# A hybrid encoder layer: first tiles in a hand-written order, another routing order, and the fourth expert pair's weights loaded in the order in which the first pair leaves its blocks

## The chip, the core and the metric

The kernel runs on one core of one Trainium2 chip. The metric is the device time of one execution in microseconds. The kernel before was timed three times: 592.09, 594.92 and 598.53 us, median 594.92 us. One further execution was profiled, and everything read from the trace is of that one.

## What is computed

512 tokens of 1024 features go through one post-norm encoder layer. What matters here of the reference:

```python
def reference(x, positions, ln_emb_g, ln_emb_b, w_in, ...):
    h = layer_norm(x, ln_emb_g, ln_emb_b)
    proj = h @ w_in[l]
    qa, ka, va, cq, ckv, kr = jnp.split(proj, IN_SPLITS, axis=-1)
    ...
    out_a = windowed_gqa_sink(qa, ka, va, a_sink[l])
    qb = (rms_norm(cq, q_a_norm_g[l]) @ w_q_b[l]).reshape(b, s, B_HEADS, 96)
    kv = (rms_norm(ckv, kv_a_norm_g[l]) @ w_kv_b[l]).reshape(b, s, B_HEADS, 128)
    ...
    out_b = mla_attention(q_nope, q_rope, k_nope, k_rope, v_b)
    mixed = jnp.concatenate([rms_norm(out_a, ...), rms_norm(out_b, ...)], axis=-1) @ w_out[l]
    h = layer_norm(DEEPNORM_ALPHA * h + mixed, ln_attn_g[l], ln_attn_b[l])
    ffn = hierarchical_moe(h, ...)   # 32 experts, each token goes to two of them
    h = layer_norm(DEEPNORM_ALPHA * h + ffn, ln_ffn_g[l], ln_ffn_b[l])
```

An expert is `silu(t @ w_gate[e]) * (t @ w_up[e]) @ w_down[e]` with 256 hidden features: 2 MB of gate and up weights and 1 MB of down weights in float32. All 32 experts are used, so 96 MB of weights are read.

## The kernel before, in words

**Start and projection.** The tokens lie in four tiles of 128 (`z[0]` to `z[3]`). Each is loaded in two halves of 512 features (`load_x`), its mean and variance are taken on DVE (`ln_stats`), and `layer_norm` applies mean, factor, gain and bias in four DVE operations per tile, with gain and bias broadcast over 128 partitions (`lng`, `lnb`, 1 MB together, loaded on SP's queue behind the first tile). PE transposes the tile in two groups of four 128x128 blocks (L257), and `split` makes of each group a rounded high half (`hth`, a cast on ACT, L208) and a low half (`htl`, a subtraction on DVE, L209). A product is three matmuls: high by high, high by low, low by high. The weights `w_in` come in four column chunks; a chunk is four loads of 512 KB (`wf`, L161), split into `wh` (ACT) and `wl` (POOL for the first chunk, DVE for the others). The first chunk's 24 matmuls of tile 0 (L385) take the high weights first; all other tiles use `mm3` (L213 to L215).

**Attention.** The low-rank vectors are expanded to queries, keys and values of the eight MLA heads in two column halves `c` of four tokens' tiles `t` each: `heads` transposes and splits, and L497 and L323 to L332 scale and rotate the queries. Behind them come scores (maximum `bnm` on DVE, L574; exponential `pr` on ACT, L577), values, the output projection, and the second LayerNorm. Up to here a scheduler, which simulates the engines, sets the order of instructions on each engine; priorities given in the source only help it.

**Routing and experts.** From the last part of the output projection on, everything is issued in the order in which it is written (`manual_schedule`). Tiles are handled in the order 0, 1, `a`, `b`; for each: logits (`logits`), choice of experts (`route`), counting (`count`), slots (`place`), selection matrix (`sel0_`), and a matmul that gathers the chosen rows, transposed (`gather`, L1109). The experts run in 16 pairs, 64 slots each, side by side on the array. One pair: 8 blocks `j` of gate and up weights, 16 matmuls in the program (the trace shows two records for each; L1243, `gates`), the activation (`gated`), 8 matmuls of down weights (L1263, `down`), and the result added to the rows `xg`, which a scatter writes to memory (`leave_rows`). The weights lie in a ring of six slots (`RING`); while pair p runs, pair p+3 is loaded into the two slots that p leaves. SP issues these loads in order: first expert's gate and up weights, second's (`load_gus`, L692), then the down weights (L709, L712). In slots 0 and 1 the first half of gate and up weights (blocks 0 to 3) is two tiles of 512 KB and the second half one of 1 MB; in the other slots both halves are 1 MB. The slots 0 and 1 hold the pairs 0, 3, 6, 9, 12 and 15. In pair 0, a group of small matmuls for the first places (L1368) stands behind the first two blocks of the gates. The end takes the last pair's result by a matmul instead of a scatter (L1310), adds the rows that were scattered, and applies the last LayerNorm.

Of the kernel before, what the change touches and what calls it, by code (L numbers as in the profile page):

```python
# [12 lines left out]
F32 = mybir.dt.float32  # L13
# [58 lines left out]
def build(tc, A, out):  # L72
# [24 lines left out]
    with top:  # L97
# [38 lines left out]
        def bvec(pl, src, n, name):  # L136
            t = pl.tile([P, n], F32, name=name)
            SY.dma_start(out=t, in_=src.partition_broadcast(P))
            return t
        load_x(0)  # L140
        lg, lb = [lp.tile([P, D], F32, name=nm) for nm in ("lng", "lnb")]
        for n in range(2):
            for dst, nm in ((lg, "ln_emb_g"), (lb, "ln_emb_b")):
                SY.dma_start(out=dst[:, 512 * n:512 * n + 512], in_=A[nm][512 * n:512 * n + 512].partition_broadcast(P))
        SY.dma_start(out=cst, in_=A["cst"][:, :C_KEEP])

        nch = [-1]

        def chunk_load(pieces):
# [4 lines left out]
            for q in range(4):  # L154
# [10 lines left out]
                split(wf[:, :, :n], wh[:, :, :n], wl[:, :, :n], PO if nch[0] == 0 else V)  # L165
# [32 lines left out]

        def layer_norm(src, dst, g, b):
            mv, rs = ln_stats(src)  # L200
            for i in range(2):
                sl = slice(512 * i, 512 * i + 512)
                V.scalar_tensor_tensor(dst[:, sl], src[:, sl], mv[:, 0:1], g[:, sl], ALU.subtract, ALU.mult)
                V.scalar_tensor_tensor(dst[:, sl], dst[:, sl], rs, b[:, sl], ALU.mult, ALU.add)
# [43 lines left out]
        for t in range(NT):  # L248
            if t == 0:
                chunks.append(chunk_load([(768, 512)]))  # L250
            elif t + 1 < NT:
                load_x(t + 1)
            layer_norm(xs[t], z[t], lg, lb)
            for kk in range(2):
                pt = ptr()
                for k in range(4):
                    PE.transpose(pt[:, k * P:(k + 1) * P],  # L257
                                 z[t][:, (4 * kk + k) * P:(4 * kk + k + 1) * P], ident)
                pv = pt.rearrange("p (a b) -> p a b", a=4)
                o = (slice(None), slice(4 * kk, 4 * kk + 4), slice(t * P, (t + 1) * P))  # L260
                split(pv, hth[o], htl[o])
# [112 lines left out]
        def chunk(ch, first=False):  # L374
            n, hs = ch
            for t in range(NT):
                pp = pproj()
                if first and t == 0:
                    ts_ = slice(t * P, (t + 1) * P)
                    O = []  # L380
                    for q in range(4):
                        O += [(k, a_, 0) for a_ in (hth, htl) for k in (2 * q, 2 * q + 1)]
                    O += [(k, hth, 1) for k in range(NK)]
                    for i, (k, a_, l) in enumerate(O):
                        PE.matmul(pp, a_[:, k, ts_], hs[k // 2][l][:, k % 2], start=(i == 0), stop=(i == 3 * NK - 1))  # L385
                    yield t, pp
                    continue
# [15 lines left out]
        for t, pp in chunk(chunks[0], True):  # L403
# [59 lines left out]
        scr = pool(p2, "p2s", bufs=2, side="right")  # L463

        def heads(src, hi, lo, c, t):
# [4 lines left out]
            split(pt[:96].rearrange("p (a b) -> p a b", a=4), hi[o], lo[o])  # L470

        for c in range(2):
            wh, wl = kv0 if c == 0 else wprep(w2, A["w_kv_b"][0], gkv, 2, 512 * c, 512)
            for t in range(NT):
# [12 lines left out]
        for c in range(2):  # L487
            wh, wl = wprep(w2, A["w_q_b"][0], gq, 6, 384 * c, 384)
            for t in range(NT):
# [9 lines left out]
                heads(qt_, qth, qtl, c, t)  # L499
# [1111 lines left out]
```

## Time and profile before

| what | value |
|---|---|
| median of 3 timed runs | 594.92 us (592.09 to 598.53) |
| the profiled execution, its own time | 591.33 us |
| its span, first to last instruction | 589.5 us |
| busy share of the span: PE, DVE, ACT, POOL | 89%, 55%, 38%, 17% |
| mean granted TensorE clock | 0.970 |

The time of the profiled execution is 1.8 us longer than its span, and the median is 0.6% above it. A busy share is a mean over stages. PE has idle time in the first 20 us, around 155 us, between 320 and 340 us and behind 548 us. A row of the timeline gives the start, the duration of a group of like instructions, the engine, the line, the operation with its output and inputs, and in brackets the idle time of the engine before it with what released it. SPq is SP's queue of DMA issues; its durations are those of the issuing, waits between issues included, not of the transfers.

### The profile page before, as it was taken

What the parts mean: (1) busy time and instruction counts of PE and PEld (TensorE: products, weight loads), DVE (VectorE), ACT (ScalarE), POOL (GpSimd) and SP (SyncE); (2) the same over time, 40 slices, a digit from 0 to 9 for tenths busy, and PEclk for the clock granted to TensorE, in tenths of its full rate; (3) what the DMA queues carried; (4) which work ended last, traced back from release to release, by engine and by line L of the source; (5) the groups of instructions that cost most, each with busy time, mean ns of one, the idle gap of its engine ahead of it and who ended that gap; (6) DMA issues with size and microseconds to landing.
All of it is one profiled execution on the core that took longest, in us unless ns stands there. A gap on an engine that the chain in (4) does not pass through costs nothing. (4 is left out here: it accounts for less than half of the span.)

```text
span 589.5 us, 8004 instructions
## 1 busy us (share of the span) xinstructions
PE 523.4 (89%) x2756; PEld 331.8 (56%) x2757; DVE 322.6 (55%) x882; ACT 222.1 (38%) x477; POOL 99.9 (17%) x141
## 2 busy tenths in 40 slices
PE   2899999999898999999998899999998699979860
PEld 1688898789766777677777444343433234323230
DVE  4946463775688757947768734434524222202177
ACT  2256451564597738856731312111111111101032
POOL 1700221311100000213200201123111101000051
PEclk9999999999899999999999989999999889989985
DMA  8983310221201005991266799999999999999663
GB/s 279 280 290 81 102 43 0 59 81 42 85 16 58 1 1 212 289 367 39 66 258 259 280 391 410 420 415 415 411 417 400 421 418 391 412 420 416 264 267 142
DMA packets 46268, 141.76 MB, mean 240 GB/s; under 512 B 12380, under 2 KB 19420, under 8 KB 37009
## 3 DMA queue, kind: packets, MB, share of 16 engines
q1 hardware_dynamic: 40608, 131.06, 58.5%
q0 software_dynamic: 4464, 8.06, 3.6%
q10 hardware_dynamic: 1152, 2.10, 0.9%
q8 instruction: 23, 0.38, 0.3%
q14 instruction: 21, 0.16, 0.1%
HBM read 133.14 MB, written 16.25 MB: 253 GB/s over the span
## 5 line engine op out<-in xcount | busy, mean ns | idle before, releaser
L1243 PE MATMUL p_gu<-w_gu,xT 128*64 128x512 f32 x512 | 125.0, 613 | 15.0 <-DMA w_gu<-in_w_gu 14.1
L1243 PEld LDWEIGHTS p_gu<-w_gu,xT 128*64 128x64 f32 x512 | 39.6, 141 | 95.6 <-issue 70.0
L1247 ACT ACTIVATE hid<-p_gu 128x256 f32<-128x256 f32 x16 | 6.1, 384 | 176.0 <-PE p_gu L1243 163.9
L1248 DVE TENSOR_TENSOR hid<-hid,p_gu 128x256 f32<-128x256 f32 x16 | 6.7, 421 | 113.9 <-ACT hid L1247 113.8
L1263 PE MATMUL p_y<-w_dn,hidT 128*64 128x512 f32 x256 | 59.9, 611 | 1.0 <-issue 0.6
L1276 DVE SCALAR_TENSOR_TENSOR xg<-p_y,wsl,xg 128x512 f32<-128x512 f32 x30 | 22.5, 751 | 28.4 <-PE p_y L1263 26.5
L1263 PEld LDWEIGHTS p_y<-w_dn,hidT 128*64 128x64 f32 x256 | 17.5, 140 | 31.4 <-issue 29.3
L604 PE MATMUL ptr<-cst,pr 128*128 128x128 f32 x208 | 33.3, 278 | 1.9 <-ACT pr L562 1.4
L1034 POOL DMA_INDIRECT xg<-norm_rows,tok x16 | 16.5, 1032 | 104.5 <-PE p_y L1263 16.8
L1269 POOL DMA_INDIRECT moe_rows<-xg,idx x15 | 15.6, 1039 | 95.0 <-DVE xg L1276 69.6
L604 PEld LDWEIGHTS ptr<-cst,pr 128*128 128x128 f32 x208 | 24.9, 145 | 9.5 <-ACT pr L562 3.2
L577 ACT ACTIVATE pr<-pmm,bnm 128x512 f32<-128x512 f32 x32 | 22.0, 689 | 10.6 <-DVE bnm L574 9.7
L574 DVE TENSOR_REDUCE bnm<-pmm 128x1 f32<-128x512 f32 x32 | 21.9, 687 | 5.3 <-PE pmm L215 4.8
L215 PE MATMUL pmm<-wh,htl 128*128 128x512 f32 (+1 forms) x64 | 24.0, 374 | 0.0
L213 PE MATMUL pmm<-wh,hth 128*128 128x512 f32 (+1 forms) x64 | 23.8, 372 | 0.0
L214 PE MATMUL pmm<-wl,hth 128*128 128x512 f32 (+1 forms) x64 | 23.5, 368 | 0.0
L562 ACT ACTIVATE pr<-pr,rc 128x512 f32<-128x512 f32 (+2 forms) x32 | 20.6, 645 | 4.1 <-DVE rc L560 3.9
L590 DVE CUSTOM_DVE_ANT_0 sm<-pmm,mask,nsink 128x256 f32<-128x256 f32 (+1 forms) x32 | 17.4, 545 | 7.6 <-PE pmm L587 6.5
L215 PE MATMUL pwo<-wh,htl 128*128 128x512 f32 (+1 forms) x56 | 20.7, 370 | 0.0
L214 PE MATMUL pwo<-wl,hth 128*128 128x512 f32 (+1 forms) x56 | 20.5, 367 | 0.0
L213 PE MATMUL pwo<-wh,hth 128*128 128x512 f32 (+1 forms) x56 | 20.5, 367 | 0.0
L1232 ACT ACTIVATE xg<-xg,of 128x1024 f32<-128x1024 f32 x15 | 17.2, 1149 | 8.5 <-PE p_x L1228 7.8
(349 smaller groups left out, 1161.6 us busy)
## 6 DMA issues: line engine op xcount, KB each, us to landing
w_gu<-in_w_gu SPq DMA_DIRECT2D x52, 1024.0 KB
w_dn<-in_w_dn SPq DMA_DIRECT2D x20, 1024.0 KB
w_gu<-in_w_gu SPq DMA_DIRECT2D x24, 512.0 KB
w_dn<-in_w_dn SPq DMA_DIRECT2D x24, 512.0 KB
wf<-in_w_in SPq DMA_DIRECT2D x12, 512.0 KB
moe_rows<-zr SPq DMA_DIRECT2D x8, 512.0 KB
rows<-moe_rows SPq DMA_DIRECT2D x8, 512.0 KB
wf<-in_w_q_b SPq DMA_DIRECT2D x12, 192.0 KB
```

Source lines behind the costliest of these rows:

```text
L213: PE.matmul(ps, ah, bh, start=first, stop=False)
L214: PE.matmul(ps, ah, bl, start=False, stop=False)
L215: PE.matmul(ps, al, bh, start=False, stop=last)
L562: SC.mul(pr[:, :n], pr[:, :n], rc)
L574: V.tensor_reduce(nm, sp, AX.X, ALU.max, negate=True)
L577: exps_.append(SC.activation(pr[:, :S], sp, AF.Exp, bias=nm, accum_out=den).ins)
L590: V.tensor_tensor_reduce(sm[:, :nk], sp[:, :nk], mask[:, mo:mo + nk], 1.0, nsink[:, h:h + 1], ALU.add, ALU.min, nm)
L604: PE.transpose(pt[:, k * P:(k + 1) * P], pr[:, k * P:(k + 1) * P], ident)
L1232: SC.mul(pl["xg"], pl["xg"], pl["of"])
L1243: PE.matmul(pg[64 * i:64 * i + 64], xT[:, j, 64 * i:64 * i + 64], ws[i][0][j], start=(j == 0), stop=(j == 7))
L1263: r = PE.matmul(py[64 * i:64 * i + 64, :], hT[:, j, 64 * i:64 * i + 64], ws[i][1][n][:, j], start=(j == 0), stop=(j == 1))
L1276: V.scalar_tensor_tensor(y, py, pl["wsl"], y, ALU.mult, ALU.add)
```

## The change

The start has other data and another order. Gain and bias of the first LayerNorm come as a small transposed table `geT` (64 bytes per partition) on ACT's DMA queue, with the constants. A tile is only normalised (one ACT operation per half, `scaled_x`), transposed, and gets gain and bias per 128x128 block after the transpose (`gain_x`, on DVE or ACT), into `hf`, from which `high` (ACT) and `low` (DVE) are made. The low halves of the first chunk's weights move from POOL to DVE (`w_low`). Tiles 0 and 1 with their 24 matmuls each stand in a hand-written order:

```diff
-            layer_norm(xs[t], z[t], lg, lb)
...
+        def scaled_x(t, kk):
...
+            SC.activation(z[t][:, sl], xs[t][:, sl], AF.Identity, scale=rs, bias=nb)
...
+        def gain_x(t, kk, ks, eng):
...
+                    SC.activation(hf[:, k], pt[:, k * P:(k + 1) * P], AF.Identity, scale=g_, bias=b_)
...
+                    V.tensor_scalar(hf[:, k], pt[:, k * P:(k + 1) * P], g_, b_, ALU.mult, ALU.add)
...
+        def w_low(q):
+            V.tensor_tensor(chunks[0][1][q][1], wfs[q], f32v(chunks[0][1][q][0]), ALU.subtract)
...
+        with tc.manual_schedule(engines={V.engine, SC.engine, PE.engine, PO.engine}):
+            stats_half(0, 0)
+            stats_half(0, 1)
+            stats_end(0)
+            stats_shift(0)
             for kk in range(2):
...
+                scaled_x(0, kk)
+                turn_x(0, kk)
+            gain_x(0, 0, range(4), V)
+            w_high(0)
...
+            w_high(2)
+            first_mm(0, hth, 2, 0)
+            first_mm(0, htl, 2, 0)
+            for kk in range(2):
+                scaled_x(1, kk)
+                turn_x(1, kk)
```

ACT's rows show the start's order. `hth` is a tile's rounded half, `wh` one of the first chunk's four rounded weights. Before:

```order
L208 CAST hth<-ptr 128x4x128
L208 CAST wh<-wf 128x1024
L208 CAST hth<-ptr 128x4x128
L208 CAST wh<-wf 128x1024 x3
L208 CAST hth<-ptr 128x4x128 x2
```

and now:

```order
L271 ACTIVATE z_64<-xt,ln_nb_158,ln_rs 128x512 x2
L298 CAST wh<-wf 128x1024
L284 ACTIVATE hf<-ptr,geT 128x128
L292 CAST hth<-hf 128x4x128
L284 ACTIVATE hf<-ptr,geT 128x128
L298 CAST wh<-wf 128x1024
L292 CAST hth<-hf 128x4x128
L298 CAST wh<-wf 128x1024
L271 ACTIVATE z_65<-xt,ln_nb_205,ln_rs 128x512 x2
L298 CAST wh<-wf 128x1024
L292 CAST hth<-hf 128x4x128
```

The two halves of tile 0 are now normalised ahead of everything else on ACT, some of the gains stand between the casts, and tile 1's two normalisations (`z_65`) stand between the third and the fourth weight cast.

The z that the later residual needs gets its gain and bias in the query projection. Two loads of 512 KB (`lgb`) are issued on SP's queue at the second half's key projection, and two DVE operations per tile and half stand behind each low half of the queries:

```diff
+                for dst, nm in zip(lgb, ("ln_emb_g", "ln_emb_b")):
+                    SY.dma_start(out=dst, in_=A[nm].rearrange("(a b) -> a b", a=2).partition_broadcast(P))
...
+                with tc.issue_after(heads(qt_, qth, qtl, c, t)):
+
+                    zt = z[t][:, 512 * c:512 * c + 512]
+                    V.tensor_tensor(zt, zt, lgb[0][:, c], ALU.mult)
+                    V.tensor_tensor(zt, zt, lgb[1][:, c], ALU.add)
```

DVE's rows show it at the first scores, where the second half's queries end (`qtl` is a low half of queries, `rp` a rotation, `bnm` the maximum of a row of scores, `rc` and `pr` a softmax's end). Before:

```order
L209 TENSOR_TENSOR qtl<-ptr,qth 96x4x128
L574 TENSOR_REDUCE bnm<-pmm 128x1
L323 SCALAR_TENSOR_TENSOR rp_1615<-pwo,rq_337,ctb 128x128
L331 SCALAR_TENSOR_TENSOR rp_1616<-pwo,rq_337,stb 128x4x16 x2
L209 TENSOR_TENSOR qtl<-ptr,qth 96x4x128
L323 SCALAR_TENSOR_TENSOR rp_1649<-pmm,rq_338,ctb 128x128
L331 SCALAR_TENSOR_TENSOR rp_1650<-pmm,rq_338,stb 128x4x16 x2
L560 RECIPROCAL rc<-den 128x1
L574 TENSOR_REDUCE bnm<-pmm 128x1
L564 TENSOR_SCALAR pr<-pr,rc 128x512
```

and now:

```order
L584 TENSOR_TENSOR qtl<-ptr,qth 96x4x128
L619 TENSOR_TENSOR z_64<-z_64,ln_emb_g 128x512
L695 TENSOR_REDUCE bnm<-pmm 128x1
L441 SCALAR_TENSOR_TENSOR rp_1676<-pwo,rq_426,ctb 128x128
L449 SCALAR_TENSOR_TENSOR rp_1677<-pwo,rq_426,stb 128x4x16 x2
L584 TENSOR_TENSOR qtl<-ptr,qth 96x4x128
L619 TENSOR_TENSOR z_65<-z_65,ln_emb_g 128x512
L620 TENSOR_TENSOR z_64<-z_64,ln_emb_b 128x512
L441 SCALAR_TENSOR_TENSOR rp_1712<-pmm,rq_427,ctb 128x128
L449 SCALAR_TENSOR_TENSOR rp_1713<-pmm,rq_427,stb 128x4x16 x2
L681 RECIPROCAL rc<-den 128x1
L620 TENSOR_TENSOR z_65<-z_65,ln_emb_b 128x512
```

Four operations on z now stand in this stretch, between the maxima on which the exponentials wait; four more follow behind it.

In the routing, the gain and bias of one half of tile `a` move ahead of the logits, `route(a)` is cut into five steps and a rest, and `place`, `count`, `sel0_` and `gather` of tile `a` move back behind `route(b)`; the row numbers and selection of the second group (`rows_of`, `select_tile`) come ahead of the exponentials:

```diff
-        steps(route(a))
-        place(1)
+        ra = route(a)
+        steps(ra, 5)
         turn(b, 0)
```

The first pair's gates go through the blocks in the order 4 to 7, 0 to 3, its places still behind the first two blocks; the factors of the rows (`residual`, `places_weights`) and the transposes for the second pair (`columns`) move between the matmuls of `down` and the DVE operations that take their result:

```diff
         def gu_tiles(slot, i):
-            if i == 0 and slot < 2:
-                return [(f"gu{slot}0{q}", 2 * q, 2) for q in range(2)]
+            if i == 1 and slot < 2:
+                return [(f"gu{slot}1{q}", 4 + 2 * q, 2) for q in range(2)]
             return [(f"gu{slot}{i}", 4 * i, 4)]
...
+        def load_turns(e, slots):
+
+            ws = [{}, {}]
+            for h in (1, 0):
+                for ts in zip(*[gu_tiles(sl, h) for sl in slots]):
+                    for i in range(2):
+                        tag, j, n = ts[i]
+                        ws[i].update(zip(range(j, j + n), load_blocks(e + i, slots[i], tag, j, n)))
...
+                if p == 0:
+                    ws[p + 3] = [(gu, None) for gu in load_turns(e, (s0, s1))]
...
+                order = 4, 5, 6, 7, 0, 1, 2, 3
+                gates(pg, xT, ws[p], order, 0, 2)
+                first_rows()
+                gates(pg, xT, ws[p], order, 2)
...
+            def between():
+
                 for i in range(2):
                     columns(plc[1], i, nx)
+                residual(0)
```

SP's rows show the loads of the fourth pair. A tile of 128x1024 is 512 KB, one of 128x2048 is 1 MB. Before, slot 0's three tiles and then slot 1's three:

```order
L692 DMA w_gu000_3971<-in_w_gu 128x1024
L692 DMA w_gu001_3973<-in_w_gu 128x1024
L692 DMA w_gu01_3975<-in_w_gu 128x2048
L692 DMA w_gu100_3977<-in_w_gu 128x1024
L692 DMA w_gu101_3979<-in_w_gu 128x1024
L692 DMA w_gu11_3981<-in_w_gu 128x2048
```

and now, with the slot as the first digit of the name, the half as the second and the quarter as the third:

```order
L817 DMA w_gu010_4038<-in_w_gu 128x1024
L817 DMA w_gu110_4040<-in_w_gu 128x1024
L817 DMA w_gu011_4042<-in_w_gu 128x1024
L817 DMA w_gu111_4044<-in_w_gu 128x1024
L817 DMA w_gu00_4046<-in_w_gu 128x2048
L817 DMA w_gu10_4048<-in_w_gu 128x2048
```

The two slots now take turns, and the second halves (blocks 4 to 7) come ahead of the first. For the pairs 6, 9, 12 and 15 the loads still go slot by slot, but in each the 1 MB tile is now the first and the two of 512 KB follow.

## Rows read from the trace of the kernel before

**Rows 1.** Windows: us, then busy us (instructions) per engine, PEclk, DMA share, GB/s

```profile
10.00:20.00 10.00, 6.34 (x18) 4.03 (x19) 8.86 (x13) 5.17 (x6) 6.74 (x4) 1.00 0.93 311
60.00:70.00 10.00, 10.00 (x52) 8.26 (x51) 4.08 (x9) 4.40 (x11) 1.37 (x3) 1.00 0.16 46
400.00:500.00 100.00, 90.36 (x428) 35.56 (x423) 32.35 (x90) 14.83 (x21) 15.81 (x15) 0.97 1.01 411
```

**Rows 2.** Timeline 0 to 18 us, DVE, POOL, ACT: start, us, idle before

```profile
5.53 0.15 DVE L181 TENSOR_SCALAR rsq_t<-ln_mv 128x1 f32<-128x1 f32 x1
5.77 0.55 POOL L183 TENSOR_TENSOR ln_rs<-rsq_t,mhalf 128x1 f32<-128x1 f32 x1 [4.56 <-DVE rsq_t L181]
...
8.01 0.75 DVE L203 SCALAR_TENSOR_TENSOR z<-xt,ln_mv,lng 128x512 f32<-128x512 f32 x1 [2.32 <-DMA lng<-in_ln_emb_g]
...
10.41 0.23 DVE L348 CAST identr<-cst 128x128 fp32r<-128x128 f32 x1
...
17.18 1.04 ACT L208 CAST wh<-wf 128x1024 fp32r<-128x1024 f32 x1 [0.30 <-DMA wf<-in_w_in]
```

**Rows 3.** Timeline of PE, 10 to 26 us

```profile
10.53 1.95 PE L257 MATMUL ptr<-cst,z 128*128 128x128 f32 x8 [10.53 <-DMA cst<-cst]
...
13.23 1.22 PE L385 MATMUL pwo<-wh,hth 128*128 128x512 f32 x2 [0.76 <-ACT wh L208]
...
19.75 1.09 PE L257 MATMUL ptr<-cst,z 128*128 128x128 f32 x4 [2.10 <-DVE z L204]
...
24.91 1.09 PE L385 MATMUL pwo<-wl,hth 128*128 128x512 f32 x4
```

**Rows 4.** Costliest groups by form: busy us, mean ns | idle before

```profile
L209 DVE TENSOR_TENSOR wl<-wf,wh 128x1024 fp32r<-128x1024 f32 x8 | 9.9, 1254 | 1.8 <-ACT wh L208 1.8
L484 DVE TENSOR_SCALAR vb<-pwo,rq 128x256 f32<-128x256 f32 x4 | 1.9, 471 | 0.0
L1122 DVE TENSOR_TENSOR z<-z,lngb 128x512 f32<-128x512 f32 x2 | 1.4, 684 | 0.0
...
L208 ACT CAST wh<-wf 128x1024 fp32r<-128x1024 f32 x12 | 12.4, 1056 | 2.2 <-DMA wf<-in_w_in 1.4 <-PE pmm L215 0.3 <-issue 0.3
L1114 ACT ACTIVATE z<-z,ln_nb,ln_rs 128x512 f32<-128x512 f32 x2 | 1.5, 806 | 0.9 <-DVE ln_nb L1119 0.9
```

**Rows 5.** Timeline 156 to 158 us, PE and DVE

```profile
156.47 0.50 PE L213 MATMUL pmm<-kth,qth 96*128 96x512 f32 x1 [1.71 <-ACT pr L577]
...
157.46 0.69 DVE L574 TENSOR_REDUCE bnm<-pmm 128x1 f32<-128x512 f32 x1
```

**Rows 6.** Windows, columns as in rows 1

```profile
130.00:150.00 20.00, 19.97 (x122) 19.37 (x121) 10.93 (x27) 8.78 (x17) 2.60 (x4) 1.00 0.20 59
155.00:160.00 5.00, 3.54 (x15) 2.91 (x16) 4.90 (x14) 2.68 (x8) 0.91 (x2) 0.78 0.54 180
330.00:338.00 8.00, 6.24 (x34) 2.49 (x33) 6.16 (x38) 0.85 (x2) 3.28 (x3) 1.00 0.64 186
342.00:350.00 8.00, 8.00 (x46) 3.67 (x44) 4.11 (x10) 1.63 (x2) 1.02 (x1) 0.99 1.02 399
```

**Rows 7.** Timeline of the first pair, PE, then SP's queue

```profile
326.92 1.94 PE L1243 MATMUL p_gu<-w_gu,xT 128*64 128x512 f32 x8 [0.78 <-DVE gn L892]
...
330.66 5.37 PE L1243 MATMUL p_gu<-w_gu,xT 128*64 128x512 f32 x24
...
328.88 9.21 SPq L692 DMA_DIRECT2D w_gu<-in_w_gu  x6
342.55 3.01 SPq L709 DMA_DIRECT2D w_dn<-in_w_dn  x4
```

**Rows 8.** Timeline of the last pair, SP's queue, then PE

```profile
525.76 12.78 SPq L692 DMA_DIRECT2D w_gu<-in_w_gu  x6
...
548.16 1.02 PE L1243 MATMUL p_gu<-w_gu,xT 128*64 128x512 f32 x2
550.38 7.39 PE L1243 MATMUL p_gu<-w_gu,xT 128*64 128x512 f32 x30 [1.20 <-DMA w_gu<-in_w_gu]
```

More of the change, by code (lines that the diff above doesn't have):

```diff
@@ L139, in bvec @@
             return t
+        geT = cp.tile([P, 2, NK], F32, name="geT")
+        SC.dma_start(out=cst, in_=A["cst"][:, :C_KEEP])
+        SC.dma_start(out=geT, in_=A["ge_T"])
         load_x(0)
[L141 to L145, printed above, removed]
         nch = [-1]
+        wfs = []
         def chunk_load(pieces):
@@ L247, in build @@
         chunks = []
[L248 to L252, printed above, removed]
-            layer_norm(xs[t], z[t], lg, lb)
-            for kk in range(2):
[L255 to L261, printed above, removed]
+        chunks.append(chunk_load([(768, 512)]))
@@ L262, in build @@
+        for t in range(2, NT):
+            for i in range(2):
+                stats_half(t, i)
+            stats_end(t)
+            stats_shift(t)
+            for kk in range(2):
+                scaled_x(t, kk)
+                turn_x(t, kk)
+                if kk:
+                    gain_x(t, kk, range(4), SC)
+                else:
+                    gain_x(t, kk, range(4), V)
+                high(t, kk)
+                low(t, kk)
         lnst.close()
@@ L372, in build, with chunk @@
         scr0, scr, scr1 = [pool(p1, nm, bufs=2, side="right") for nm in ("p1s0", "p1s", "p1s1")]
-        def chunk(ch, first=False):
+        def chunk(ch, first=()):
             n, hs = ch
             for t in range(NT):
+                if t < len(first):
+                    yield t, first[t]
+                    continue
                 pp = pproj()
[L378 to L387, printed above, removed]
                 for k in range(NK):
@@ L1209, in build @@
         for t in (1, a, b):
+            rows_of(t)
+        sels[1] = [select_tile(2, t) for t in range(NT)]
+        for t in (1, a, b):
             exps(t)
@@ L1256, in gated, with down @@
             return hT
-        def down(hT, ws, put):
+        def down(hT, ws, put, between=None):
+            pys = []
             for n in range(2):
@@ L1264, in down @@
                                       ws[i][1][n][:, j], start=(j == 0), stop=(j == 1))
-                put(slice(512 * n, 512 * n + 512), py)
+                pys.append(py)
+                if not between:
+                    put(slice(512 * n, 512 * n + 512), py)
+            if between:
+                between()
+                for n in range(2):
+                    put(slice(512 * n, 512 * n + 512), pys[n])
             return r.ins
@@ L1276, in put @@
                 V.scalar_tensor_tensor(y, py, pl["wsl"], y, ALU.mult, ALU.add)
-            r = down(hT, ws, put)
+            r = down(hT, ws, put, between)
             scatter(pl)
```

207 lines of the change are left out of this document (145 added, 62 removed).

## The prediction

> **What bounds the kernel now.** I read the windows first, because a busy share over the whole span mixes stages. From 60 to 70 us PE is busy all of 10.00 us at a DMA share of 0.16; from 400 to 500 us the DMA share is 1.01 at 411 GB/s while PE is busy 90.36 of 100 us [rows 1]. So the projections are bound by PE and the expert stage by the stream of weights: 1 MB takes 2.55 us at 411 GB/s, and a pair of experts (6 MB) some 15 us. Work saved on PE counts only ahead of the expert stage, and behind its beginning only bytes per time count. Between these stages the change touches four places: the start, the first scores, the fill of the fourth pair's slots, and the last pair. I took each from its own timeline.
>
> **The start, before.** PE does nothing until 10.53 us, when the constants land; from 10 to 20 us it is busy 6.34 of 10 us [rows 1, 3]. DVE has the variance at 5.53 and POOL the factor 0.55 us later, but DVE waits 2.32 us, until 8.01, for the broadcast gain [rows 2]. The second gap on PE is 2.10 us ahead of 19.75, waiting for tile 1's z [rows 3]. Also PE is slow: the two matmuls of the group at 13.23 take 1.22 us, those at 24.91 four in 1.09. A group's last matmul ends some 0.4 us after the next could start, so they follow each other at about 0.5 us at first and at 0.23 later. I count PE work at the later pace: 0.13 us per transpose, 0.23 per matmul. Until 24.6 us the trace has 16 transposes and 15 matmuls, 16 x 0.13 + 15 x 0.23 = 5.5 us of work. At 24.6 PE is 24.6 - 5.5 = 19.1 us behind an engine that works from 0; from there it loses nothing.
>
> **The start, after.** Parts: the 1 MB broadcast goes, the constants come first on another queue, tile 0 needs no gain before its transposes. The normalisation on ACT is 0.81 us per 128x512 (L1114) [rows 4]. The factor is there at 5.77 + 0.55, the shift some 0.5 us later, so ACT normalises from about 6.9 and PE transposes from 7.75. The gain per 128x128 block isn't in the trace in this form; its bounds are 0.23 us (a cast of 128x128 on DVE at 10.41) and 0.47 (L484, twice as wide, from PSUM) [rows 2, 4]. I take 0.27, near the row of the same size. Four on DVE, 1.1 us, lie beside ACT's first weight cast of 1.06 us [rows 4], so the first matmul comes near 10.65 instead of 13.23. The low weight halves cost DVE 1.25 us each [rows 4] and lie behind the first matmuls, which don't need them. The weights themselves are no bound: before, ACT waited 0.30 us on each [rows 2], and 1 MB ahead of them is gone, 3.4 us at 311 GB/s [rows 1].
>
> The bound is then ACT, and the place to look at is tile 1. Its normalisation stands behind the third weight cast, needs a factor which DVE reaches only behind tile 0's gains and two loads' waits, and holds the fourth cast behind it. Followed row by row through the order, ACT stands idle from 13.7 to 16.0 and PE gets two gaps, 0.85 and 0.6 us, between 16 and 18.6. So PE loses: 7.75 before the first transpose; 0.95 between transposes and first matmul; 1.45 in the two gaps. If it keeps the slow pace until 18.6, as long as it is fed in pieces, the busy 18.6 - 10.15 = 8.45 us are worth half, a loss of 4.2. Sum 14.35 against 19.1: **4.8 us gained**. Bounds: without the gaps and with the fast pace from 15 us, 7.75 + 0.95 + 3.1 = 11.8, a gain of 7.3; with the slow pace until 24.6, as before, 10.15 + 7.2 = 17.4, a gain of 1.7.
>
> [...]
>
> **The z operations.** Before, DVE's broadcast form costs four operations of 0.75 us per tile at the start; now sixteen of 128x512, 0.68 us each (L1122) [rows 4], stand in the query projection. The first eight, 5.5 us, fall into a stretch where PE is busy 19.97 of 20 us and DVE only 10.93 [rows 6]: nine us of cover, so nothing. If the cover were gone, they would cost their 5.5 us. The last eight stand at the first scores, where the cover is gone already: from 155 to 160 us DVE is busy 4.90 of 5 us, PE 3.54, at a granted clock of 0.78 [rows 6]; PE waits 1.71 us at 156.47 for an exponential, which itself waits for a maximum like that at 157.46 on DVE [rows 5]. Behind each z operation stand the maxima, in order. Upper bound: all eight count, 5.4 us. Lower bound: 0.5, if DVE's work that goes out of the way later in the attention absorbs the delay. I take about the middle, **2.5 us lost**, because four of the eight lie ahead of the maxima that PE waits for and four behind them.
>
> **The stream at pair 0.** From 330 to 338 us the DMA share is 0.64 at 186 GB/s, from 342 to 350 us 1.02 at 399 [rows 6]. The cause is the order in which SP waits: six loads are issued from 328.88 over 9.21 us [rows 7]. The gates free blocks in the order of j for both experts at once, the loads go through slot 0 first and then slot 1; so the load of slot 0's second half waits for the end of the gates (330.66 + 5.37 = 336.0 [rows 7]), and slot 1's blocks, free for some us, wait behind it. The deficit is 8 x (1 - 186/411) = 4.4 us. Now 1 MB is free after the first two blocks, 1 MB after the next two, 2 MB at the end, and SP asks for them in that order; moreover the gates begin with blocks 4 to 7, whose rows are gathered first, so they don't wait the 0.78 us for the others [rows 7]. With some 2 us less in front of the gates, 1 MB chunks of 2.55 us each nearly follow one another. I take the whole deficit, **4.4 us gained**; the lower bound is half, 2.2, as the places' 16 matmuls still stand between the first and the second MB. The factors that move behind `down` lie beside PE's wait for weights in the next pair and free no weights; I cost them at nothing, up to 1 us if the down weights' release at 342.55 [rows 7] slips.
>
> **The last pair.** For the pairs in slots 0 and 1 the loads still go slot by slot, but the 1 MB tile now comes first. The gates at 548.16 do two records and wait 1.20 us, until 550.38, for slot 1's first tile [rows 8]. That tile was the fourth of six loads [rows 8], complete at 1 + 1 + 0.5 = 2.5 MB; now it is complete at 3 MB. Half a megabyte is **1.2 us lost**, as the end depends on this pair. Lower bound 0, if the rows of the earlier pairs, not this pair, set the end.
>
> **Sum.** On the profiled execution -4.8 + 2.5 - 4.4 + 1.2 = -5.5: 591.33 becomes 585.8. The median shown is 0.6% above that execution, so I predict 589.4 against 594.92. All times below are put on the median in the same way. A difference of 1%, 5.9 us, is about what a measurement of this kernel can tell from no change.
>
> **Rivals.**
> A, chance 0.20: the slow pace at the start lasts as before. For it: the pace doubled only after PE had worked without a break from 19.75 on [rows 3], and the new order has gaps until 18.6. Against it: the gaps are smaller. The start then gives 1.7: -2.4, 592.4 us. [...]
> B, chance 0.22: the start gives 7.3 and the attention absorbs all but 0.5 of the z operations: -10.0, 584.9 us. For it: z's last eight operations have DVE work behind them that can slip; against it: DVE is full at 4.90 of 5 us [rows 6].
> C, chance 0.13: half of the dip stays, because the places still split the gates: -3.3, 591.5 us.
> D, chance 0.10, slower: the DVE queue blocks. The z operations are in line with everything else on DVE and need two new broadcast loads; if these land late, as the broadcast of 8.01 did [rows 2], or if the scheduler's covers fail, all sixteen delay what PE waits for, 16 x 0.68 = 10.9 us instead of 2.5: -4.8 + 10.9 - 4.4 + 1.2 = +2.9, 597.8 us. It decides from the twelfth uncovered operation on, where 8.0 us lost equal the gains. Against it: the loads have the DMA queues at a share of 0.20 [rows 6].
>
> **How the numbers follow.** The forecast has the chance 0.35, with a range of its own from 587 to 592. From B's bounds to D's, 582 to 597 holds 8 in 10. Faster by over 1% means below 589.0: half of the forecast's chance, all of B's and little of the others, 0.43; slower by over 1% is D and some of what I have not seen, 0.09; 0.48 remain.
>
> **What would show it.** Right: the first matmul near 10.7 us and the fast pace by 19; a DMA share near 1 in the 8 us behind the first pair's first blocks; PE's wait in the last pair some 1.2 us longer. Wrong at the start: PE still spaced at 0.5 us at 22. Wrong at the scores: idle PE growing by more than 5 us between 150 and 170, or none at all. The whole is wrong if the expert stage begins earlier and the end does not move with it: then something else than the fill of the fourth pair holds the stream.

## The result and the profile after

The changed kernel takes 598.51 us (median of 18 runs) against 594.49 us of the kernel before (18 runs): the ratio is 1.0070, with a 95% interval from 1.0048 to 1.0093. It is slower by 0.7%, some 4 us, where 0.9% faster was forecast; the measured time lies outside the predicted range of 582 to 597. The profiled execution of the changed kernel took 600.57 us. It stands 2 us above its median, the one of before 3 us below; so the two profiles are 9.4 us apart in span and the medians 4.0. Times of single rows below come from one execution each; what counts for a verdict are the ratios.

**The start.** PE in the first 21 us, as [rows 3]:

```profile
7.76 1.97 PE L276 MATMUL ptr<-cst,z 128*128 128x128 f32 x8 [7.76 <-ACT z L271]
10.99 1.22 PE L309 MATMUL pwo<-wh,hth 128*128 128x512 f32 x2 [1.26 <-ACT hth L292]
...
14.57 1.05 PE L309 MATMUL pwo<-wh,hth 128*128 128x512 f32 x2
16.15 0.73 PE L309 MATMUL pwo<-wh,htl 128*128 128x512 f32 x2 [0.53 <-DVE htl L295]
17.73 1.36 PE L276 MATMUL ptr<-cst,z 128*128 128x128 f32 x8 [0.84 <-ACT z L271]
19.37 0.73 PE L309 MATMUL pwo<-wh,hth 128*128 128x512 f32 x2 [0.28 <-ACT wh L298]
19.94 0.62 PE L309 MATMUL pwo<-wh,htl 128*128 128x512 f32 x2
...
24.63 0.73 PE L309 MATMUL pmm<-wh,hth 128*128 128x512 f32 x2 [0.40 <-ACT hth L292]
```

The transposes begin at 7.76, the first matmul at 10.99 (forecast 7.75 and 10.65). Two gaps of 0.53 and 0.84 us stand where two were expected, and two small ones of 0.28 and 0.40 behind them. Two matmuls still take 1.05 us at 14.57 and 0.62 from 19.94 on; the groups between take 0.73. The projection's end shows what is left of it. The first row is of before, the second of after:

```profile
107.43 0.39 PE L213 MATMUL pwo<-w2h,cth 128*128 128x512 f32 x1
```

```profile
103.91 0.39 PE L209 MATMUL pwo<-w2h,cth 128*128 128x512 f32 x1
```

The first matmul of the key projection starts 3.5 us earlier.

**The scores.** The windows at the first scores, as [rows 6]: first from 150 to 155 us of the kernel before, then two of the changed one; and POOL's rotation sum in the query projection:

```profile
150.00:155.00 5.00, 4.75 (x30) 4.26 (x28) 1.85 (x8) 1.64 (x4) 1.66 (x4) 1.00 0.26 50
```

```profile
150.00:155.00 5.00, 2.73 (x17) 1.91 (x15) 3.66 (x9) 2.69 (x6) 2.08 (x5) 1.00 0.48 144
155.00:160.00 5.00, 4.30 (x15) 3.01 (x15) 5.00 (x12) 1.95 (x4) 1.35 (x2) 0.59 0.31 105
```

```profile
139.35 0.46 POOL L450 TENSOR_TENSOR qtok<-rp,rp 128x128 f32<-128x128 f32 x1 [6.20 <-DVE rp L449]
141.19 2.94 POOL L450 TENSOR_TENSOR qtok<-rp,rp 128x128 f32<-128x128 f32 x1 [1.38 <-DVE rp L449]
```

PE is busy 2.73 of 5 us from 150 to 155 instead of 4.75, DVE is full from 155 to 160 (4.90 of 5 us before), and the granted clock falls to 0.59 (0.78 in [rows 6]). A rotation sum on POOL (`qtok`) that takes 0.46 us takes 2.94 us beside a train of DVE operations.

**The first two pairs.** PE, then POOL's gather of the second pair's rows, in the changed kernel and before, and SP's next loads, as [rows 7]:

```profile
327.03 1.94 PE L1380 MATMUL p_gu<-w_gu,xT 128*64 128x512 f32 x8
...
331.01 5.37 PE L1380 MATMUL p_gu<-w_gu,xT 128*64 128x512 f32 x24
...
338.94 3.65 PE L1401 MATMUL p_y<-w_dn,hidT 128*64 128x512 f32 x16 [0.52 <-DVE hidT L1391]
346.91 1.85 PE L1364 MATMUL p_x<-cst,xg 128*128 128x128 f32 x8 [4.32 <-DMA xg<-norm_rows,tok]
...
352.32 9.52 PE L1380 MATMUL p_gu<-w_gu,xT 128*64 128x512 f32 x32
```

```profile
336.52 1.27 POOL L1168 DMA_INDIRECT xg<-norm_rows,tok  x1 [18.39 <-PE p_gu L1380]
```

```profile
335.41 1.01 POOL L1034 DMA_INDIRECT xg<-norm_rows,tok  x1 [0.31 <-DVE wc L910]
```

```profile
329.00 8.21 SPq L817 DMA_DIRECT2D w_gu<-in_w_gu  x6
340.90 3.02 SPq L843 DMA_DIRECT2D w_dn<-in_w_dn  x4
358.44 4.71 SPq L817 DMA_DIRECT2D w_gu<-in_w_gu  x4
```

The first pair starts at 327.03, as before: the start's gain is gone by then. Its gates take the same times as before, 1.94 and 5.37 us. Then PE waits 4.32 us for the rows of the second pair (`xg<-norm_rows,tok`), whose gather was issued at 336.52. That is the first of four gathers; before, the first pair's came first and the second pair's second, at 335.41. The change also exchanged these two, which the section on the change does not say. The second pair's gates start at 352.32 instead of 345.98, and they take 9.52 us for the same 32 records that took 7.09: from 348 to 356 us the granted clock is 0.50 (1.00 before, from 346 to 354). SP's next loads, which need this pair's blocks, begin at 358.44 instead of 349.66. The windows of the stream:

```profile
330.00:338.00 8.00, 6.39 (x35) 2.64 (x34) 6.90 (x46) 3.10 (x12) 1.27 (x1) 1.00 1.04 419
342.00:350.00 8.00, 3.68 (x20) 3.12 (x16) 0.69 (x1) 1.79 (x3) 0.00 (x0) 0.81 1.00 369
348.00:356.00 8.00, 7.74 (x30) 5.17 (x30) 4.40 (x13) 2.72 (x3) 0.82 (x1) 0.50 0.44 179
350.00:362.00 12.00, 11.74 (x44) 4.95 (x44) 3.71 (x12) 1.07 (x2) 1.10 (x1) 0.70 0.36 122
```

and the second pair's gather in the DMA view of before (issues from 335.2 to 336 us) and of the changed kernel (336.2 to 337); the last number is the time from issue to landing:

```profile
xg<-norm_rows,tok POOLq DMA_INDIRECT x1, 6.9
```

```profile
xg<-norm_rows,tok POOLq DMA_INDIRECT x1, 10.3
```

This gather lands after 10.3 us instead of 6.9; the medians of all four are 10.8 and 7.7. The dip of [rows 6] is gone: 419 GB/s from 330 to 338 us instead of 186. But from 350 to 362 us the stream runs at 122 GB/s, where the kernel before has 398. A hole of 4.4 us was closed, and one of 12 x (1 - 122/411) = 8.4 us opened behind it.

**The last pair**, as [rows 8]:

```profile
556.00 1.02 PE L1380 MATMUL p_gu<-w_gu,xT 128*64 128x512 f32 x2
559.75 7.08 PE L1380 MATMUL p_gu<-w_gu,xT 128*64 128x512 f32 x30 [2.73 <-DMA w_gu<-in_w_gu]
```

PE waits 2.73 us for the first tile of slot 1 instead of 1.20.

### The profile page after: what moved, and what is told of

It is laid out like the page before. It is cut to its first block, busy times and chain, and to the rows that moved or that the text cites. A ratio compares the mean times of both kernels' runs of the same rounds, so it can differ in the third digit from the quotient of the medians.

```text
span 598.9 us, 8037 instructions
## 1 busy us (share of the span) xinstructions
PE 528.9 (88%) x2756; PEld 332.3 (55%) x2757; DVE 328.8 (55%) x910; ACT 232.9 (39%) x497; POOL 91.0 (15%) x137
## 5 line engine op out<-in xcount | busy, mean ns | idle before, releaser
L1401 PE MATMUL p_y<-w_dn,hidT 128*64 128x512 f32 x256 | 58.5, 598 | 1.6 <-issue 0.6
L1420 DVE SCALAR_TENSOR_TENSOR xg<-p_y,wsl,xg 128x512 f32<-128x512 f32 x30 | 22.4, 751 | 24.6 <-PE p_y L1401 23.9
L1401 PEld LDWEIGHTS p_y<-w_dn,hidT 128*64 128x64 f32 x256 | 17.2, 136 | 31.0 <-issue 28.2
L1364 PE MATMUL p_x<-cst,xg 128*128 128x128 f32 x120 | 19.4, 288 | 4.3 <-DMA xg<-norm_rows,tok 4.3
L1364 PEld LDWEIGHTS p_x<-cst,xg 128*128 128x128 f32 x120 | 13.9, 145 | 16.5 <-issue 13.3
L211 PE MATMUL pmm<-wh,htl 128*128 128x512 f32 (+1 forms) x56 | 20.8, 372 | 0.0
L1368 ACT ACTIVATE xg<-xg,of 128x1024 f32<-128x1024 f32 x15 | 17.2, 1148 | 8.8 <-PE p_x L1364 8.5
L210 PE MATMUL pmm<-wl,hth 128*128 128x512 f32 (+1 forms) x56 | 20.5, 367 | 0.0
```

The costliest lines, as they stand in the source:

```text
L210: PE.matmul(ps, ah, bl, start=False, stop=False)
L211: PE.matmul(ps, al, bh, start=False, stop=last)
L1364: PE.transpose(pt[:, k], pl["xg"][:, P * (4 * j2 + k):P * (4 * j2 + k) + P], ident)
L1401: r = PE.matmul(py[64 * i:64 * i + 64, :], hT[:, j, 64 * i:64 * i + 64], ws[i][1][n][:, j], start=(j == 0), stop=(j == 1))
L1420: V.scalar_tensor_tensor(y, py, pl["wsl"], y, ALU.mult, ALU.add)
```

## The experiments

Each ratio is to the kernel before on the same chip, with its 95% interval.

**z's operations ahead of the scores (e1).** The two loads go to the first key projection, four of the sixteen operations to the second, twelve to the first half's queries:

```diff
-                    zt = z[t][:, 512 * c:512 * c + 512]
-                    V.tensor_tensor(zt, zt, lgb[0][:, c], ALU.mult)
-                    V.tensor_tensor(zt, zt, lgb[1][:, c], ALU.add)
+                    if c == 0:
+                        zgain(t, 0, 1)
+                        zgain(t, 1, 0)
+                        zgain(t, 1, 1)
```

> The changed kernel with its sixteen z operations moved ahead of the first scores: four stand in the second half's key projection, twelve in the first half's query projection; nothing else differs. Theory Z (the eight operations at the first scores cost their full 5.4 us there, because every one of them delays a maximum on which PE waits): PE's busy time from 150 to 155 us returns from 2.7 to above 4.5 us, the first pair's gates start about 5 us earlier than 327.0, and the time falls from 598.5 to about 593.5. Rival (the attention absorbs the delay, and the loss seen there comes from the earlier start alone): the gates start within 2 us of 327.0 and the time stays above 596.5.

Measured: 593.91 us, ratio 1.0008 (0.9980 to 1.0035). The time is as Theory Z said, but its way is not: PE is busy 3.44 of 5 us from 150 to 155 and not above 4.5, and the profiled execution, at 600.66 us far above the median, has the first gates at 331.8 and not at 322, so the whole of that profile can't stand for the median. What it does show is a new price at the old place:

```profile
139.76 1.95 POOL L450 TENSOR_TENSOR qtok<-rp,rp 128x128 f32<-128x128 f32 x1 [5.93 <-ACT w2h L477]
142.21 3.10 POOL L450 TENSOR_TENSOR qtok<-rp,rp 128x128 f32<-128x128 f32 x1 [0.50 <-DVE rp L449]
```

```profile
157.50 0.64 PE L580 MATMUL ptr<-cst,qtok 128*96 128x128 f32 x4 [1.62 <-POOL qtok L450]
```

With twelve operations among the queries, two rotation sums on POOL take 1.95 and 3.10 us, and PE waits 1.62 us for POOL. The operations are dear in the query projection as well, not only at the scores.

**z's operations in the projection (e6).** The loads go on ACT's queue behind the first tiles, the operations into the second and third column chunk:

```diff
+            with tc.issue_after(low_rank(t, pp, 1)):
+                zgain(t, 0, 0)
+                zgain(t, 0, 1)
+                zgain(t, 1, 0)
...
             rope(kr_, pp[:, 32:160].rearrange("p (a b) -> p a b", a=2), tabk, t, 2, 32, scr)
+            zgain(t, 1, 1)
```

> The changed kernel with z's sixteen operations moved to the second and third column chunk of the projection, where neither PE nor POOL waits for DVE; the two broadcast loads go on ACT's queue behind the first tiles. Theory Z2 (the z operations cost what they do because they stand among query and score work: they fill DVE, and POOL's half-microsecond rotation sums beside them last up to 3 us): the rotation sums (qtok on POOL) take 0.46 us each again, PE is busy above 4.5 of 5 us from 146 to 151, the first pair's gates start near 322 instead of 327, and the time falls from 598.5 to about 593.5. Rival (the ramp of the scores costs the same whatever stands on DVE): gates within 2 us of 327.

Measured: 592.79 us, ratio 0.9983 (0.9955 to 1.0011). POOL's eight rotation sums as a group, before, changed and here:

```profile
L332 POOL TENSOR_TENSOR qtok<-rp,rp 128x128 f32<-128x128 f32 x8 | 4.4, 553 | 26.3 <-DVE rp L331 19.0 <-PE pmm L215 5.8 <-DVE rc L560 0.8
```

```profile
L450 POOL TENSOR_TENSOR qtok<-rp,rp 128x128 f32<-128x128 f32 x8 | 7.4, 923 | 27.9 <-DVE rp L449 23.8 <-ACT pr L698 2.7 <-DVE rc L681 1.4
```

```profile
L450 POOL TENSOR_TENSOR qtok<-rp,rp 128x128 f32<-128x128 f32 x8 | 4.4, 551 | 26.9 <-DVE rp L449 19.5 <-PE pmm L211 5.8 <-DVE rc L691 0.8
```

The mean is back from 923 to 551 ns, PE is busy 4.81 of 5 us from 146 to 151, the first gates are at 320.45, and the ratio falls by 0.87%, 5.2 us, with the intervals clear of each other. Theory Z2 holds, in its sign and its size. The 320.45 alone proves little: e7, below, has the same program up to there but for the place of a few tiles, and its first gates are at 324.31 (the granted clock from 150 to 200 us averages 0.93 in e7 and 0.97 in e6). This run also does not separate what the sums on POOL cost from what the scores cost; the part on the prediction comes back to that.

**The old loads (e2).** Only the load order, the tiles of slots 0 and 1 and the first pair's block order go back:

```diff
-                if p == 0:
-                    ws[p + 3] = [(gu, None) for gu in load_turns(e, (s0, s1))]
-                else:
-                    ws[p + 3] = [(load_gus(e, s0), None), (load_gus(e + 1, s1), None)]
+                ws[p + 3] = [(load_gus(e, s0), None), (load_gus(e + 1, s1), None)]
...
-                order = 4, 5, 6, 7, 0, 1, 2, 3
+                order = range(NK)
```

> The changed kernel with the fourth pair's loads, the tiles of the slots 0 and 1 and the first pair's block order as before; all else as changed. Theory C (collision: the full stream of weights delays the gather of the second pair's rows, and PE waits for them): the gather lands some 7.5 us after its issue instead of 10.8, PE's wait of 4.3 us ahead of the second pair's transposes falls below 1.5, that pair's gates start 3 to 5 us earlier and run at the full pace (7.1 us instead of 9.5), the transfer rate from 330 to 338 us falls below 300 GB/s again, and the time falls to about 594.5. Rival O (order: what was put between the down matmuls and their taking delays the second pair by itself): the wait stays above 3 us and the time above 597.

Measured: 592.26 us, ratio 0.9983 (0.9956 to 1.0009), 0.87% below the changed kernel. PE at the second pair:

```profile
342.08 1.06 PE L1364 MATMUL p_x<-cst,xg 128*128 128x128 f32 x8 [0.18 <-PE p_y L1401]
...
345.18 8.79 PE L1380 MATMUL p_gu<-w_gu,xT 128*64 128x512 f32 x32
```

The wait of 4.32 us is gone and the gates start 7.1 us earlier than in the changed kernel. Theory C's sign holds, and the time falls by more than it said. The median of the four gathers fell to 9.2 us only, not to 7.5; the second pair's own, the one that PE waits for, fell from 10.3 to 6.7. The gates still took 8.79 us, at a granted clock of 0.81, with no wait ahead of them.

**The old order within the first pair (e3).** `residual`, the places' weights and `columns` back to where they stood, loads as changed.

> The changed kernel with the residual factors, the places' weights and the second pair's transposes where they stood before (behind the activation and behind the down matmuls' results); loads as changed. Theory C: the gather still lands more than 10 us after its issue, PE still waits 3 us or more for it, and the time falls by at most 2.5 us, to 596 or more. Rival O: the second pair's gates start near 347 instead of 352.3 and the time falls to about 591.5.

Measured: 597.25 us, ratio 1.0040 (1.0011 to 1.0068). PE still waits 2.77 us for the gather, a little less than the 3 of Theory C; the second pair's gather takes 10.6 us, and the second gates start at 349.92. Rival O falls: the order is worth at most some 2 us, and the intervals of this run and of the changed kernel overlap.

**All of the first pair as before, z's operations as in e1 (e5).**

> The changed kernel with z's operations moved as in the first of these runs and with all of the first pair as before (load order, tiles, block order, order of the gathers, residual factors and transposes); what is left of the change is the new start and the new routing order. If the start's gain of about 3.5 us and the routing's of about 2 us reach the end, the time is 594.5 - 5.5 = 589. Rival (a start earlier by itself does not move the stream of weights): 593 or more.

Measured: 598.35 us, ratio 1.0073 (1.0041 to 1.0105): a miss by 9 us. It has e1's stretched sums, and it puts back two things more than e2: the order of e3 within the pair, and the order of the gathers, so that the second pair's rows are gathered behind the first pair's. In its profile PE waits 3.34 us for them: the first pair's gather landed 4.4 us after its issue, the second pair's, issued 1.58 us later, 8.7. The second gates take 9.01 us. With the old routing and z's operations in the projection, the same order of the gathers leaves no wait (e10, below). So the old loads by themselves do not keep PE from waiting; what made the whole dearer than e1 was not tried part by part.

**The loads alone in the kernel before (e8).**

> The kernel before with only this part of the change: the fourth pair's loads in turns, second halves first, the tiles of slots 0 and 1 cut the other way, the first pair's blocks in the order 4 to 7, 0 to 3. Theory C (collision): from 330 to 338 us the stream runs at 370 GB/s or more, the gather of the rows lands 10 us or more after its issue instead of 7.2, PE waits 2.5 us or more for it ahead of the second pair, and the time is 3 to 4 us above that of before. The prediction on record for this part was the other way: 4.4 us faster, less 1.2 at the last pair, so 591.

Measured: 594.15 us, ratio 1.0016 (0.9989 to 1.0043). Neither number is right: the loads alone change nothing that can be measured. The gather's median is 8.8 us, and PE goes from `down` to the second pair without a wait. The stream shows why nothing is won:

```profile
330.00:338.00 8.00, 6.20 (x33) 2.45 (x33) 6.19 (x38) 0.38 (x1) 3.45 (x4) 1.00 0.91 321
338.00:346.00 8.00, 8.00 (x42) 4.15 (x41) 3.02 (x7) 2.19 (x3) 0.88 (x2) 0.79 0.97 373
346.00:354.00 8.00, 7.75 (x38) 2.69 (x37) 2.35 (x9) 1.19 (x3) 0.96 (x1) 1.00 0.92 302
```

```profile
551.32 8.43 PE L1257 MATMUL p_gu<-w_gu,xT 128*64 128x512 f32 x30 [2.74 <-DMA w_gu<-in_w_gu]
```

The dip of 186 GB/s becomes 321, but the next 16 us run at 373 and 302, where the kernel before has 388 and 388. The second pair's gates start at 346.07, as before, so the stream, which got its bytes earlier, waits earlier for the next free slots. And the last pair waits 2.74 us instead of 1.20.

**z early and the old loads (e7), then turns for the later pairs (e9).** e7 is e6 with the loads of e2. e9 also loads the pairs 6, 9, 12 and 15 in turns, with the first halves first (`load_turns` now takes `h` in the order 0, 1, not shown):

```diff
-                ws[p + 3] = [(load_gus(e, s0), None), (load_gus(e + 1, s1), None)]
+                if p and s0 == 0:
+                    ws[p + 3] = [(gu, None) for gu in load_turns(e, (s0, s1))]
+                else:
+                    ws[p + 3] = [(load_gus(e, s0), None), (load_gus(e + 1, s1), None)]
```

> The run before (z's operations in the projection) with the fourth pair's loads, tiles and the first pair's block order as before, too. If the price of the full stream (the late gather, some 5 us) and that of the z operations (some 5 us) add up, the time is about 598.5 - 10 = 588.5, below the kernel before. If the start's gain is used up in the stream's fill, whatever the load order, it stays at 592 or more.

> The second of these runs with the loads of the pairs 6, 9, 12 and 15 in turns (both slots' first quarters, second quarters, then the halves), so that a pair's first tiles are complete after 1 MB instead of 2.5. If the last pair's wait is on the path to the end, as the prediction's last term says, PE's wait in the last pair (1.2 us before, 2.7 changed) falls below 0.5 us and the time by 1 to 2.5 us against the run it is made from; if the end hangs on the stream's last bytes or on the scattered rows, it is the same within 1 us.

Measured: e7 589.71 us, ratio 0.9931 (0.9892 to 0.9969); e9 587.60 us, ratio 0.9904 (0.9866 to 0.9941). Against the changed kernel e7 is 1.4% faster; the two prices together would be 1.7%. Against e6 it is 0.5% faster, with overlapping intervals, so the price of the loads is clear of noise only in e2. e9 has the lowest median of this study, 1% below the kernel before, from six runs. Its last pair:

```profile
542.76 3.60 PE L1390 MATMUL p_gu<-w_gu,xT 128*64 128x512 f32 x16
546.60 1.04 PE L1390 MATMUL p_gu<-w_gu,xT 128*64 128x512 f32 x2 [0.23 <-DMA w_gu<-in_w_gu]
548.99 3.65 PE L1390 MATMUL p_gu<-w_gu,xT 128*64 128x512 f32 x14 [1.35 <-DMA w_gu<-in_w_gu]
```

The first 16 records run at once; the waits, 0.23 and 1.35 us, have moved to later tiles. The ratio fell by 0.27%, within both intervals: that the last pair's first tile sets the end was not shown.

**Turns at the first pair, too (e11).**

> The run with turns for the pairs 6 to 15 (587.6 us) with turns for the fourth pair, too: the dip of the stream at the first pair is filled and the last pair's first tiles are early. Theory C: the rate from 330 to 338 us or the 8 us behind the first blocks rises above 360 GB/s, the rows' gather lands 10 us or more after its issue, PE waits 1.5 us or more for it, the stream loses behind it what it won, and the time is 588 to 590.5, not better. Rival (the fill of the dip pays, and only the last pair's tiles hid it): 585.5 or less.

Measured: 589.76 us, ratio 0.9942 (0.9905 to 0.9980). (The halves go in the order 0, 1 here, and the first pair's blocks from 0 to 7.) It is not better than e9, as Theory C said, but by another way than it said: 360 GB/s from 330 to 338 us and 312 from 346 to 354, with the gathers' median at 10.3 us and no wait of PE for them, as its `down` takes 5.35 us instead of 3.65 (a granted clock of 0.86 from 330 to 338 us). The hole moved, as in e8.

**The start alone (e10) and e9 with the old routing (e12).**

> Only the new start, with z's operations in the projection; routing order, first pair and all loads as before. If the start's 3.5 us (the projection ends at 103.6 instead of 107.1) pass through to the end, the time is 591 against 594.4 of before. If the expert stage's fill takes them back, 594.

> The run with turns for the pairs 6 to 15 (587.6 us) with the routing order of before. If the new routing order is worth what the trace shows (from the output projection's end to the first gates 11.4 to 12.4 us instead of 13.7), the time is 1 to 2 us longer, 589. If the write and gather of the second pair's rows set the pace there, whose write came 1.3 us later with the new order, it is the same within 0.7 us or shorter.

Measured: e10 590.30 us, ratio 0.9944 (0.9916 to 0.9972): the start's 3.5 us reach the end. e12 593.09 us, ratio 0.9975 (0.9944 to 1.0006), 0.7% above e9, with the intervals just apart: beside the turns the new routing order helps. But e7 and e10, which differ in the routing order and in the order within the first pair, are 0.13% apart, far inside their intervals; so what the routing order is worth by itself stays open.

## Why the prediction failed

**The fill of the fourth pair: the step that failed.** The prediction says "I take the whole deficit, **4.4 us gained**". The loads by themselves gained nothing in the kernel before (e8: 594.15 us against 594.44), and in the changed kernel taking them back gained 0.87%, 5.2 us (e2). The term took the dip as bytes lost for good. A dip between two releases of slots is not. From the first pair's gates, which free two slots, to the second pair's, which free the next two, SP can load one pair, 6 MB, which takes 15.3 us at 2.55 us per MB. If the second gates start 19 us behind the first, 3.8 us of the stream are lost wherever the hole stands. Here is the stretch from the first gates' start to 10 us behind the second's, for before, changed, e3, e8 and e2:

```profile
326.92:355.98 29.06, 26.92 (x142) 12.93 (x144) 15.65 (x74) 7.89 (x18) 5.29 (x5) 0.94 0.90 334
```

```profile
327.03:362.32 35.29, 28.52 (x127) 13.58 (x126) 14.48 (x70) 6.26 (x16) 5.37 (x5) 0.85 0.79 294
```

```profile
326.32:359.92 33.60, 28.80 (x132) 13.52 (x132) 14.82 (x72) 6.74 (x17) 5.28 (x5) 0.85 0.85 315
```

```profile
326.29:356.07 29.78, 27.14 (x143) 12.84 (x144) 16.43 (x75) 7.89 (x18) 5.29 (x5) 0.94 0.95 346
```

```profile
327.12:355.18 28.06, 25.67 (x128) 11.28 (x129) 14.23 (x70) 6.85 (x17) 5.36 (x5) 0.94 0.93 351
```

| run | first to second gates, us | less 15.3 | lost, length x (1 - rate/411) |
|---|---|---|---|
| before | 19.1 | 3.8 | 5.4 |
| changed | 25.3 | 10.0 | 10.0 |
| e3 | 23.6 | 8.3 | 7.8 |
| e8 | 19.8 | 4.5 | 4.7 |
| e2 | 18.1 | 2.8 | 4.1 |

The loss follows the distance of the gates. With the loads in turns (changed, e3, e8) it is within 0.5 us of the third column, and with the old loads (before, e2) 1.3 to 1.6 us above it: that much the turns do save at the same distance. The other runs are like that: with turns (e1, e6, e11) within 1 us, with the old loads (e5, e7, e9, e10, e12) 0.4 to 3.4 us above. The distance moves the loss by more, 6 us in the changed kernel. So the term was to be read from what starts the second pair: its rows, which are written to memory, read back by the gather and transposed. The prediction didn't follow that chain. These are the writes on ACT's queue, before and changed:

```profile
319.39 5.63 ACTq L825 DMA_DIRECT2D norm_rows<-z  x3
```

```profile
324.60 1.69 ACTq L959 DMA_DIRECT2D norm_rows<-z  x2
```

The last of them is issued by 326.3 instead of 325.0, as the new routing puts tile `b`'s z later. The first gather is issued at 336.52 instead of 333.83, the second pair's at 336.52 instead of 335.41 (the row numbers are there 2 to 3 us ahead of the first gather in both, so I take the write's landing as what it waits for; that was not tested). It takes 10.3 us instead of 6.9, beside a stream of 359 GB/s instead of 287 meanwhile. The old loads (e2), or the new loads in the old order of everything else (e8), leave PE with hardly a wait. Both changes together make the second pair late in the changed kernel, e3 and e6 (waits of 4.32, 2.77 and 2.27 us); in e1, where the first pair's later 24 records of gates took 7.07 us instead of 5.37 at a granted clock of 0.79, and in e11, where `down` took 5.35 us instead of 3.65, both are there and PE does not wait. A slower first pair alone does not decide it: `down` took 5.35 us in e3, too. The granted clock adds to it: 0.50 behind the wait, where the second pair's gates take 9.52 us instead of 7.09. How much of the 5.2 us is the gather and how much the clock was not separated. The prediction had a smaller gain as rival C, "half of the dip stays"; none of its rivals let the full stream itself delay PE.

**z's operations: the mechanism right, the size wrong.** The prediction named the place, DVE full at the first scores, and took 2.5 us, "about the middle" of 0.5 and 5.4. Measured by e6 it is 5.2 us, close to the upper bound. Where it is lost can be read from the first matmul of the scores, before and changed:

```profile
153.37 0.48 PE L213 MATMUL pmm<-kth,qth 96*128 96x512 f32 x1
```

```profile
150.60 0.48 PE L209 MATMUL pmm<-kth,qth 96*128 96x512 f32 x1
```

It starts 45.94 us behind the first matmul of the key projection before, and 46.69 us changed. So the part called free, "nine us of cover, so nothing", cost 0.75 us, and the rest is lost at the scores, as the prediction's upper bound has it: PE waits 2.27 us at 154.25 for the exponential, 1.71 before, and from 150 to 170 us the granted clock averages 0.83 instead of 0.91. Idle PE alone would not have shown it: from 150 to 170 us it grew by 1.8 us (busy 16.50 of 20 us, 18.29 before), not by the 5 that the prediction named as a sign. In the covered part, DVE's idle time covers the operations, but POOL's sums lie beside them and stretch (2.94 us instead of 0.46). PE waits 0.20 us for that sum in the changed kernel, and 1.62 us for another in e1. POOL's sum in the changed kernel, from 141.19 to 144.13, lasts about as long as a train of five DVE operations beside it, from 140.94 to 143.81; what holds it was not tested apart.

**The start: the mechanism right, 3.5 us instead of 4.8.** PE's gaps are larger than the sum took: 1.26 us ahead of the first matmul for 0.95, and 0.53 + 0.84 + 0.28 + 0.40 = 2.05 behind it for 1.45, together 0.9 us. But the slow pace ends sooner than the 18.6 of the sum, which was the author's assumption and which no run shows: in the changed kernel the matmuls start 0.43 us apart up to 14.99 us and 0.23 apart from 19.71 on, and in e6, e7 and e9 to e12 the slow groups of 1.05 us end between 15 and 17.2 us. Before, they are 0.43 apart up to 24.68 and 0.23 from there on. The trace's records of the clock begin at 15.92 us in the changed kernel and at 24.66 before, both with 1.00; a stretch ahead of the first record shows as 1.00 in the column, too, so the 1.00 of [rows 1] from 10 to 20 us is no record of the clock there. In the changed kernel PE is busy at the slow pace 1.97 us from 7.76 on and 4.63 us from 10.99 to 15.62. That is 6.6 us, of which half is lost, 3.3 instead of 4.2, and that makes up for the gaps. What the sum left out lies behind 24.6, where it said that nothing is lost: counted by its matmuls and transposes, at 0.23 and 0.13 us each, PE is some 4.0 us of work ahead of the kernel before at 26 us and some 3.4 from 30 on (four matmuls at 27.91 take 1.58 us instead of 1.09). That is 0.6 of the 1.3 us; the rest stays open. Rival A, the slow pace until 24.6, falls.

**The last pair: right in the trace, 1.5 us instead of 1.2** of added wait; what it costs in time was not shown (e9).

**The sum.** By rows: -3.5 for the start, +5.2 for z, -2.2 for the routing order and the first pair's block order, which start the first pair sooner behind the output projection (its last group starts at 312.06 before and 314.38 now, the gates at 326.92 and 327.03; with the old block order, in e2, 0.9 of the 2.2 are gone), +4.6 for the stream's loss of 10.0 against 5.4, and +1.5 at the end: +5.6, against 4.0 measured between the medians. Most of these terms are read from the two profiles, which lie 9.4 us apart, so the sum is a rough one.

```profile
312.06 1.18 PE L1094 MATMUL pwo<-woah,aol 128*128 128x512 f32 x4
```

```profile
314.38 1.17 PE L1228 MATMUL pwo<-woah,aol 128*128 128x512 f32 x4
```

## What to carry to other kernels

Closing a dip in a transfer stream that is fed through a ring gained nothing where the next release of the ring came no sooner (e8: 321 GB/s for 186, the second gates at 346.07 us for 345.98, 594.15 us for 594.44); measure from release to release, subtract the time of the bytes in between, and look for what starts the next consumer. Beside the fuller stream a small transfer landed later (here a gather, 10.3 us beside 359 GB/s for 6.9 beside 287), so the round trips that lie on the critical path (here a write, a gather, and the second pair) are to be followed first. Before idle time of an engine is counted as cover for added work on it, look whether another engine's work that someone waits for slows down beside it (here POOL's sum, 2.94 us for 0.46).

## What the runs showed of the hardware

A POOL addition of 128x128 float32 took 0.45 to 0.47 us in seven of its eight places in the kernel before and 1.21 us in the eighth; in the changed kernel one took 2.94 us beside a train of DVE operations of 0.55 to 0.68 us each, and in e1 one took 3.10, with DVE busy 5.00 of the 5 us from 140 to 145. From its issue to its landing, the gather of the second pair's rows took 6.9 us before, where the stream meanwhile ran at 287 GB/s, and 10.3 us in the changed kernel, where it ran at 359. In e9 it took 6.7 us, with 285 GB/s from 330 to 338 us; in e6 some 9 (issued at 329.24, PE goes on at 338.24), with 374 in the same window; in e3 10.6, with 372 to 382 from 334 to 346 us. e1 stands apart: with 360 GB/s from 342 to 346 us and 413 from 346 to 350, the gather issued at 341.16 had landed when PE came to it at 348.36. Behind a wait of 4.32 us on PE the granted clock was 0.50 from 348 to 356 us, and the second pair's gates took 9.52 us for the same work as the 7.09 before. It was below 1.00 behind a short wait, too: in e2, behind 0.18 us, the same gates took 8.79 us at a mean clock of 0.81. In e9, behind 0.27 us, they took 7.09 us.
